# Weight sums of twelve Strassen units made during the attention and kept in DRAM, and five more units by Strassen's scheme

## The chip, the cores and the metric

The kernel runs on one core of a Trainium2 chip. The metric is the device time of one execution in microseconds (us), as the median of several runs. Five engines work beside each other, each through its own instructions in the order of the program: TensorE (PE in the profile; PEld is its weight load), VectorE (DVE), ScalarE (ACT), GpSimd (POOL) and SyncE (SP). An instruction that waits for a semaphore holds up all that stand behind it on its engine. Here SP and POOL do little but issue DMA transfers.

## The reference

One decoder layer on 256 tokens of width 2048, in float32. Two groups of heads attend, their result goes through `w_o`, and a SwiGLU block, a gated embedding and a last norm follow. The change is about the SwiGLU block and borrows time from the attention.

```python
a = rmsnorm(h, attn_norm)
proj = a @ w_in                       # then MLA heads and MoBA heads (causal attention)
h = h + concat(out_mla, out_moba) @ w_o
f = rmsnorm(h, ffn_norm)
h = h + (silu(f @ w_gate) * (f @ w_up)) @ w_down      # D_FF = 5632
g = sigmoid(rmsnorm(h, ple_norm) @ w_ple_gate)
h = h + g * (p @ w_ple_proj)
return rmsnorm(h, final_norm)
```

## The kernel before

**Units.** All large products are cut into units, listed in program order by `group`. A unit is two blocks of 128 rows of a weight (one 1 MB piece of 256 x 1024 in the SwiGLU block) against all 256 tokens. Weights and activations are split into a high and a low part, and `three` (L349) makes each product of three matmuls: high by high, low by high, high by low. An ordinary unit has 2 row blocks x 2 column halves x 2 token halves, each of three matmuls with 512 columns: 24 matmuls. A Strassen unit treats its 256 x 1024 piece of weight and its 256 x 256 piece of activation as two by two quarters and needs seven products instead of eight: 21 matmuls (`seven`, L393). For this it needs four weight sums and four activation sums. The activation sums are made once, in `act_transpose` (L127), for the first `SEVENS` pairs of row blocks. The weight sums are made in place by VectorE for every Strassen unit (`split_lo`, L339, L342 and L343).

**The way of a weight.** SP loads it from DRAM into one of the buffers `raw0` to `raw4` (three of them during the attention, five in the SwiGLU block). ScalarE writes the high part into a ring (`split_hi`, L329; ringh, moreh, most in the profile), VectorE subtracts it from the raw data to get the low part (`split_lo`, L340; ringl, morel, most), TensorE multiplies. A buffer is free again when its last split is done, and a place in the ring when the matmuls that read it are done. So splits stand two units ahead of their matmuls in the attention, and about 11 us ahead in the SwiGLU block.

**Order.** The loop at the end of the kernel writes out the program unit by unit. For each it first calls `step()`, which moves every open task on by one piece (attention heads, norms, transposes), then emits the splits of later units whose ring places are free, then the matmuls. The sequence is: input projections (ga, q0, u0, q1, u1, qk0, qk1, v) with the attention as tasks between them; wo0 and wo1 for `w_o`; then for the five column groups ci = 0 to 4 of the SwiGLU block eight units of gate (g0 to g4) and eight of up (u0 to u4; the label u0 is used by both parts), with the down units of the group before between them; then a narrower group, the last down units, and the gated embedding.

`mixed` (L990) names the pairs of row blocks of a group in their order, with an S ahead of those that go by Strassen's scheme: two in u0, five in g1, six in g2 to g4 and u1 to u4. After the last unit of an up group VectorE adds the Strassen part to each of the four banks and multiplies it with the gate (L381 and L958, "the evacuation" below); the result is then transposed on TensorE (`ff_transpose`, L978). For ci = 1 to 4 these transposes wait in `S["turned"]` until the down units in between are done. For ci = 0 they are a task: half of them stand in the program behind the 24 matmuls of g1's first unit, half one unit later.

Of the kernel before, what the change touches and what calls it, by code (L numbers as in the profile page):

```python
# [8 lines left out]
F32 = mybir.dt.float32  # L9
# [26 lines left out]
def kernel(ctx, tc, x, p, positions, attn_norm, w_in, kv_norm, w_ukv, w_o, ffn_norm,  # L36
# [150 lines left out]
        pass  # L187

    def group(name, srcs, ks, chunks, lhs, evac, pool=None, singles=0, per=2, sums=None, sevens=(), adding=(),
              order=None, swap=False, bank0=0, deep=False, into=None):  # L190

        pairs = [ks[i:i + 1] for i in range(singles)] + [ks[i:i + per] for i in range(singles, len(ks), per)]
        st = {"banks": None, "begun": set()}
        for i, pr in enumerate(pairs):
            u = Unit()
            u.name, u.srcs, u.ks, u.chunks, u.lhs, u.st = name, srcs, pr, chunks, lhs, st
            u.first, u.last, u.evac, u.pool = i == 0, i == len(pairs) - 1, evac, pool
            u.order = order or [(c, t) for c in range(len(chunks)) for t in range(NT)]
            u.idx, u.store, u.again, u.into = i, None, None, into
            u.strassen, u.sevens_first, u.sevens_end = i in sevens, i in sevens[:1], i in sevens[-1:]  # L200
            u.mixed, u.sums, u.swap, u.bank0, u.deep, u.adding = len(sevens) > 0, sums, swap, bank0, deep, i in adding
            units.append(u)

    raw = {}
# [7 lines left out]
    def load(i):  # L212
        if i >= len(units) or units[i].again or i in raw:
            return
        u = units[i]
        u.asked = asking[0]
        n = sum(c1 - c0 for _, c0, c1 in u.srcs)
        nk = len(u.ks)
        if u.raw >= len(raws):
            raws.append(big.tile([128, 2048], F32, name=f"raw{u.raw}", tag=f"f1{'hl'[u.raw - 3]}"))  # L220
# [16 lines left out]
    def plan(wide):  # L237
# [18 lines left out]
            jobs.append(jb)  # L256
            return jb

        order = [0, 1, 2]
        back = next(i for i, u in enumerate(units) if u.name == "dl0")  # L260
        for i, u in enumerate(units):
            u.turns = []
            if u.again:
                continue
            if i == wide:
                at = 12
            if i == wide + 3:
                order = [3, 4] + order
            u.raw = order.pop(0)
            order.append(u.raw)  # L270
            nch, nk = len(u.chunks), len(u.ks)
# [34 lines left out]
        return jb.h, jb.l  # L306

    def raw_of(jb):
        f = raw[jb.unit].rearrange("q k c -> q (k c)")
# [21 lines left out]
    def split_lo(jb, c0=0, c1=None, n=1):  # L331

        if units[jb.unit].adding:
            return
        h, l, r = by_row_tile(n, *parts_of(jb), raw_of(jb))
        tt = nc.vector.tensor_tensor
        f = quarters(jb) if jb.kind == "21" else None
        if f is not None:
            tt(f[:, 0:2], f[:, 1:2].to_broadcast([128, 2, 512]), f[:, 0:4:3], op=ALU.subtract)  # L339
        tt(l[:, :, c0:c1], r[:, :, c0:c1], h[:, :, c0:c1].bitcast(F32), op=ALU.subtract)  # L340
        if f is not None:
            tt(f[:, 3], f[:, 3], f[:, 0], op=ALU.subtract)  # L342
            tt(f[:, 2], f[:, 2], f[:, 3], op=ALU.subtract)  # L343

    def split(jb):
        split_hi(jb)
# [326 lines left out]
    def after_q_mla(half):  # L673
        def g():
# [205 lines left out]
            add(g(), wait)  # L880
        return after

    SEVENS = 6

    def ffn_norm_half(k0):

        def after():
            def g():
                if k0 == 0:
                    S["nrm"] = stage_tile(1024).rearrange("q t (a b) -> q (t a) b", a=2).rearrange(  # L890
                        "q n (u v) -> q n u v", u=2)
                    sums = [big.tile([128, 2, 3, 4, 128], F32R, name=f"sums{x}", tag=x) for x in ("att", "more_sums")]
                    S["sums"] = [[x[:, i, n] for x in sums for n in range(3)] for i in range(2)]
# [59 lines left out]
    def up_evac(ci, n, nb):  # L953
        left = {"n": nb}

        def f(c, t, c0, c1, b, off=0):
# [32 lines left out]

    def mixed(name, order=((0, 0), (1, 0), (0, 1), (1, 1))):  # L990

        pairs = {'g0': '0 1 2 3 4 5 6 7', 'u0': '6 7 S0 S1 2 3 4 5', 'g1': '6 5 S0 S1 S2 S3 S4 7'}.get(name, '6 S0 S1 S2 S3 S4 S5 7').split()
        n = [int(x.strip("S+")) for x in pairs]
        sevens = tuple(i for i, x in enumerate(pairs) if x[0] == "S")
        return dict(ks=[2 * x + i for x in n for i in range(2)], chunks=C2, lhs=a_l, sums=a_sums, sevens=sevens,
                    adding=tuple(i for i, x in enumerate(pairs) if x[-1] == "+"), order=list(order) if sevens else None,
                    swap=not sevens, deep=True)

    def gate(ci):
# [228 lines left out]
        return ahead  # L1228

    nxt, j = 2, 0  # L1230
    for i, u in enumerate(units):
        asking[0] = i
        load(i + 3)
        if i < 5:
            load_x(xt, 768 + 256 * i, 1024 + 256 * i)
        if u.name == "dl0" and u.idx == 1:
# [8 lines left out]
            step()  # L1245
        for n in range(max(1, len(u.turns))):
            todo, late = [], []
            while nxt < len(jobs) and jobs[nxt].wait < j and jobs[nxt].unit <= i + (3 if i > 1 else 1) and \
# [36 lines left out]
            done = jobs[nxt].unit - 1 if nxt < len(jobs) else len(units)  # L1285
            for m in range(i + 4, min(done + 6, len(units)) if i >= wide else min(done + 4, wide + 3)):
                load(m)
            j += not u.again


# [23 lines left out]
```

## Time and profile before

| | us |
|---|---|
| time, median of 3 runs (1191.03 to 1191.93) | 1191.58 |
| the profiled execution, its own time | 1192.75 |
| its span, first to last instruction | 1191.0 |
| TensorE busy in the span | 1179.0 |
| VectorE busy | 916.2 |
| ScalarE busy | 699.7 |
| GpSimd busy | 43.4 |
| data moved by DMA | 250.30 MB |

TensorE counts as busy while a matmul is in its pipeline, so its share says that it hardly ever ran dry, not that it ran at its peak. VectorE is busy for about two thirds of the attention and almost always in the SwiGLU block, as the slices of the page show:

```
PE   9999999999999999999999999999999999999996
DVE  5644635656457678998999899989998999897474
```

In a row of a timeline the columns are the start, the busy time, engine, line, operation, output and inputs with shapes, and in brackets the idle time of the engine before it with what ended it.

### The profile page before, as it was taken

To read this page: it belongs to the slowest core of one execution; us is meant where nothing else is said; L and a number is where in the kernel's file an instruction comes from. 1 tells how busy PE (TensorE), PEld (TensorE's weight loads), DVE (VectorE), ACT (ScalarE), POOL (GpSimd) and SP (SyncE) were. 2 spreads that over 40 slices of the span, in tenths; PEclk is the share of its full clock that TensorE was granted. 3 is DMA by queue.
4 is the path that set the end of the run, shared out by engine and by line. 5 is a ranking of instruction groups with operands and counts; after the bars stand their busy time and mean duration, and the time that the engine had idled before them with its cause. 6 is when DMAs were issued, how large, how long until landed. Compare 5 with 4: busy or idle time off the path is not lost.

```text
span 1191.0 us, 14454 instructions
## 1 busy us (share of the span) xinstructions
PE 1179.0 (99%) x5501; PEld 984.1 (83%) x5501; DVE 916.2 (77%) x1076; ACT 699.7 (59%) x892; POOL 43.4 (4%) x56
## 2 busy tenths in 40 slices
PE   9999999999999999999999999999999999999996
PEld 6888888899888888888888888888888888888886
DVE  5644635656457678998999899989998999897474
ACT  6745645456556755465656565757465656465453
POOL 4300000000000000000000000000000000000000
PEclk9999999999999999999999999999999999999998
DMA  8653654435653877385867777686859586836531
GB/s 295 219 194 110 216 162 166 151 110 199 237 210 119 297 236 269 117 297 167 296 194 243 235 238 238 216 279 201 258 210 281 186 262 213 340 137 220 209 106 71
DMA packets 79734, 250.30 MB, mean 210 GB/s; under 512 B 4844, under 2 KB 9248, under 8 KB 78384
## 3 DMA queue, kind: packets, MB, share of 16 engines
q1 hardware_dynamic: 75744, 229.93, 54.1%
q0 software_dynamic: 3632, 18.93, 8.7%
q8 instruction: 43, 0.70, 0.2%
q10 hardware_dynamic: 288, 0.52, 0.1%
q14 instruction: 27, 0.22, 0.1%
HBM read 228.39 MB, written 12.58 MB: 202 GB/s over the span
## 4 chain that ended last, share of the span: by engine, by line
PE 97%; ACT 1%; DVE 1%; DMA 1%; SPq 0%; issue 0%; DVEq 0%
PE bank L353 31%; PE bank L351 31%; PE bank L352 31%; PE bank L138 1%; PE bank L978 1%; PE bank L542 1%; PE bank L663 1%; DMA x<-in_x 1%; PE bank L571 0%; PE bank L545 0%; PE bank L565 0%; DVE ringl L340 0%; ACT ringh L329 0%; ACT att L555 0%; ACT att L561 0%; PE bank L572 0%
## 5 line engine op out<-in xcount | busy, mean ns | idle before, releaser
L340 DVE TENSOR_TENSOR ringl<-raw,ringh 128x1024 fp32r<-128x1024 f32 (+4 forms) x298 | 436.5, 1483 | 133.9 <-ACT ringh L329 129.4
L329 ACT CAST ringh<-raw 128x1024 fp32r<-128x1024 f32 (+4 forms) x298 | 365.9, 1262 | 282.5 <-PE bank L352 122.9
L351 PE MATMUL bank<-ringh,aT 128*128 128x512 f32 (+3 forms) x744 | 287.4, 386 | 0.0
L353 PE MATMUL bank<-ringl,aT 128*128 128x512 f32 (+3 forms) x744 | 282.9, 380 | 0.1
L352 PE MATMUL bank<-ringh,aT 128*128 128x512 f32 (+3 forms) x744 | 282.1, 379 | 0.0
L353 PEld LDWEIGHTS bank<-ringl,aT 128*128 128x128 f32 x744 | 139.7, 188 | 27.3 <-DVE ringl L340 1.8
L352 PEld LDWEIGHTS bank<-ringh,aT 128*128 128x128 f32 x744 | 140.0, 188 | 24.7
L351 PEld LDWEIGHTS bank<-ringh,aT 128*128 128x128 f32 x744 | 140.0, 188 | 24.6 <-ACT aT L124 0.3
L329 ACT CAST moreh<-raw 128x1024 fp32r<-128x1024 f32 (+2 forms) x68 | 78.9, 1187 | 46.7 <-DVE raw L339 31.9
L340 DVE TENSOR_TENSOR morel<-raw,moreh 128x1024 fp32r<-128x1024 f32 (+2 forms) x64 | 84.1, 1328 | 1.2 <-ACT moreh L329 0.6
L351 PE MATMUL bank<-ringh,ffTh 128*128 128x512 f32 x204 | 79.4, 389 | 0.0
L352 PE MATMUL bank<-ringh,ffTl 128*128 128x512 f32 x204 | 79.4, 389 | 0.0
L353 PE MATMUL bank<-ringl,ffTh 128*128 128x512 f32 x204 | 79.4, 389 | 0.0
L329 ACT CAST most<-raw 128x1024 fp32r<-128x1024 f32 (+2 forms) x55 | 54.3, 1012 | 33.5 <-DVE raw L339 20.6
L339 DVE TENSOR_TENSOR raw<-raw 128x1024 f32<-128x1024 f32 x57 | 69.8, 1225 | 1.9
L340 DVE TENSOR_TENSOR most<-raw,most 128x1024 fp32r<-128x1024 f32 (+2 forms) x55 | 63.9, 1170 | 1.8 <-ACT most L329 1.6
L352 PEld LDWEIGHTS bank<-ringh,ffTl 128*128 128x128 f32 x204 | 38.3, 188 | 8.0
L351 PEld LDWEIGHTS bank<-ringh,ffTh 128*128 128x128 f32 x204 | 38.3, 188 | 7.9
L353 PEld LDWEIGHTS bank<-ringl,ffTh 128*128 128x128 f32 x204 | 38.3, 188 | 7.9
L343 DVE TENSOR_TENSOR raw<-raw 128x512 f32<-128x512 f32 x57 | 39.4, 692 | 2.0
L342 DVE TENSOR_TENSOR raw<-raw 128x512 f32<-128x512 f32 x57 | 39.0, 684 | 0.0
L353 PE MATMUL bank<-most,aT 128*128 128x512 f32 x86 | 33.9, 395 | 0.0
(332 smaller groups left out, 1869.0 us busy)
## 6 DMA issues: line engine op xcount, KB each, us to landing
raw<-in_w_down SPq DMA_DIRECT2D x44, 1024.0 KB, 4.9
raw<-in_w_gate SPq DMA_DIRECT2D x40, 1024.0 KB, 7.0
raw<-in_w_up SPq DMA_DIRECT2D x40, 1024.0 KB, 8.4
raw<-in_w_in SPq DMA_DIRECT2D x40, 512.0 KB, 4.1
raw<-in_w_o SPq DMA_DIRECT2D x16, 1024.0 KB, 5.2
raw<-in_w_ple_gate SPq DMA_DIRECT2D x16, 1024.0 KB, 5.0
raw<-in_w_in SPq DMA_DIRECT2D x8, 1024.0 KB, 4.9
hd<-copied POOLq DMA_DIRECT2D x8, 1024.0 KB, 9.5
```

The lines of the kernel that those rows point to most:

```text
L138: nc.tensor.transpose(b[:, (2 * i + t) * 128:(2 * i + t + 1) * 128], part[:, t, i * 128:(i + 1) * 128], ident)
L329: nc.scalar.copy(h[:, :, c0:c1], r[:, :, c0:c1])
L339: tt(f[:, 0:2], f[:, 1:2].to_broadcast([128, 2, 512]), f[:, 0:4:3], op=ALU.subtract)
L340: tt(l[:, :, c0:c1], r[:, :, c0:c1], h[:, :, c0:c1].bitcast(F32), op=ALU.subtract)
L342: tt(f[:, 3], f[:, 3], f[:, 0], op=ALU.subtract)
L343: tt(f[:, 2], f[:, 2], f[:, 3], op=ALU.subtract)
L351: nc.tensor.matmul(b, xh, h, start=start, stop=False)
L352: nc.tensor.matmul(b, xl, h, start=False, stop=False)
L353: nc.tensor.matmul(b, xh, l, start=False, stop=stop)
L542: nc.tensor.matmul(s[:, c0:c0 + nk], qT[:, q * 128:(q + 1) * 128], kT[:, 0:nk], start=True, stop=qpe is None)
L663: nc.tensor.transpose(b[:, (2 * i + t) * 128:(2 * i + t + 1) * 128], src[:, t, col(i0 + i):col(i0 + i) + 128], ident)
L978: nc.tensor.transpose(b[:, (2 * i + t) * 128:(2 * i + t + 1) * 128], st[:, t, (k + i) * 128:(k + i + 1) * 128], ident)
```

## The change

- **Five more Strassen units.** `SEVENS` is 7, so a seventh pair of row blocks gets activation sums. `mixed` gives g1 six Strassen units and u1 to u4 seven each. The groups u1 to u4 now begin with a Strassen unit.
- **Early sums.** For the last Strassen unit of g1 to g4 and the last two of u1 to u4 (12 units) a new task, `early_sums`, makes the weight sums during the attention. For each unit GpSimd issues a load of the 1 MB piece into one SBUF buffer; three steps later VectorE makes the sums in place with three instructions, and GpSimd issues a store of them to DRAM; one step later the next unit's load follows, which waits for that store. In the SwiGLU block such a unit loads 0.75 MB of the weight and 1 MB of sums into two of the five raw buffers, and its three instructions on VectorE fall away there.
- **Loads.** They are now issued by `loads`, as soon as the splits that used the same buffers before stand in the program.
- **Zeros.** The clearing of `qpT` goes from GpSimd to VectorE.
- **Transposes of ci = 0.** `up_evac` now puts them into `S["mid"]` instead of a task. The loop takes `S["mid"]` up behind the first ordinary unit of a mixed group, and u0's own last unit is one.

```diff
-                if 0 < ci < 5:
-                    S["turned"] = turned
+                if ci < 5:
+                    S["turned" if ci else "mid"] = turned
                 else:
-                    add(turned, 2 if ci else 1)
+                    add(turned, 2)
...
-    SEVENS = 6
+    SEVENS = 7
...
-        pairs = {'g0': '0 1 2 3 4 5 6 7', 'u0': '6 7 S0 S1 2 3 4 5', 'g1': '6 5 S0 S1 S2 S3 S4 7'}.get(name, '6 S0 S1 S2 S3 S4 S5 7').split()
+        pairs = {'g0': '0 1 2 3 4 5 6 7', 'u0': '6 7 S0 S1 2 3 4 5', 'g1': '6 S0 S1 S2 S3 S4 S5 7'}.get(
+            name, '6 S0 S1 S2 S3 S4 S5 7' if name[0] == 'g' else 'S0 S1 S2 S3 S4 S5 S6 7').split()
...
+                    early=sevens[-2 if name[0] == "u" else -1:] if name[-1] in "1234" else (), order=list(order) if sevens else None,
...
+    def early_sums():
+        for u in units:
+            if not u.early:
+                continue
+            f = big.tile([128, 4, 512], F32, name="wsums", tag="more_sums")
+            (w, c0, _), k0 = u.srcs[0], u.ks[0] * 128
+            nc.gpsimd.dma_start(f.rearrange("q (k a) c -> q k (a c)", k=2),
+                                w[k0:k0 + 256, c0:c0 + 1024].rearrange("(k q) c -> q k c", q=128))
+            yield 3
+            tt = nc.vector.tensor_tensor
+            tt(f[:, 0:2], f[:, 1:2].to_broadcast([128, 2, 512]), f[:, 0:4:3], op=ALU.subtract)
+            tt(f[:, 3], f[:, 3], f[:, 0], op=ALU.subtract)
+            tt(f[:, 2], f[:, 2], f[:, 3], op=ALU.subtract)
+            u.early = dram.tile([128, 2048], F32, name=f"wsums{u.name}{u.idx}")
+            nc.gpsimd.dma_start(u.early, f.rearrange("q a c -> q (a c)"))
+            yield 1
...
+        if u.early:
+            r = raws[u.raw][:, 0:1536]
+            (w, c0, _), k0 = u.srcs[0], u.ks[0] * 128
+            nc.sync.dma_start(r[:, 0:512], w[k0:k0 + 128, c0:c0 + 512])
+            nc.sync.dma_start(r[:, 512:1536], w[k0 + 128:k0 + 256, c0:c0 + 1024])
+            nc.sync.dma_start(raws[u.raw2], u.early)
...
-                nc.gpsimd.memset(qpT[64 - 64 * i:128 - 64 * i, i::2], 0.0)
+                nc.vector.memset(qpT[64 - 64 * i:128 - 64 * i, i::2], 0.0)
```

**TensorE behind u0 of the SwiGLU block.** Before, these rows stand behind the 24 matmuls of g1's first unit: L978 is the transpose of ci = 0, bank the PSUM bank that is written.

```order
L351 MATMUL bank_82<-ringh,aT_85 128x512
L352 MATMUL bank_82<-ringh,aT_86 128x512
L353 MATMUL bank_82<-ringl,aT_85 128x512
L978 MATMUL bank_77<-ident,stage 128x128 x4
L978 MATMUL bank_78<-ident,stage 128x128 x4
L351 MATMUL bank_83<-ringh,aT_85 128x512
L352 MATMUL bank_83<-ringh,aT_86 128x512
```

Now, in the changed program, the last matmuls of u0 (from the buffer most) and the first of g1 (bank_83) look so; the transposes have line L1019.

```order
L390 MATMUL bank_80<-most,aT_85 128x512
L391 MATMUL bank_80<-most,aT_86 128x512
L392 MATMUL bank_80<-most,aT_85 128x512
L1019 MATMUL bank_77<-ident,stage 128x128 x4
L1019 MATMUL bank_78<-ident,stage 128x128 x4
L1019 MATMUL bank_79<-ident,stage 128x128 x4
L1019 MATMUL bank_80<-ident,stage 128x128 x4
L390 MATMUL bank_83<-ringh,aT_85 128x512
```

All sixteen transposes moved from behind g1's first unit (and the next) to directly behind u0's last matmul.

**VectorE ahead of u0's evacuation.** Before: raw_113 and raw_114 hold g1's first two units, raw_2794 its third, which is its first Strassen unit; L381 begins the evacuation.

```order
L340 TENSOR_TENSOR ringl<-raw_113,ringh 128x1024 x2
L340 TENSOR_TENSOR ringl<-raw_114,ringh 128x1024 x2
L340 TENSOR_TENSOR ringl<-raw_2794,ringh 128x1024
L339 TENSOR_TENSOR raw_2794<-raw_2794 128x1024
L340 TENSOR_TENSOR ringl<-raw_2794,ringh 128x512
L342 TENSOR_TENSOR raw_2794<-raw_2794 128x512
L343 TENSOR_TENSOR raw_2794<-raw_2794 128x512
L340 TENSOR_TENSOR morel<-raw_2794,moreh 128x1024 x2
L381 TENSOR_TENSOR U<-U,bank_77 128x512
```

Now, with L361 for the split, L360, L363 and L364 for the sums and L420 for the evacuation, behind the first unit's pair of splits:

```order
L361 TENSOR_TENSOR ringl<-raw_114,ringh 128x1024
L360 TENSOR_TENSOR raw_114<-raw_114 128x1024
L361 TENSOR_TENSOR ringl<-raw_114,ringh 128x512
L363 TENSOR_TENSOR raw_114<-raw_114 128x512
L364 TENSOR_TENSOR raw_114<-raw_114 128x512
L361 TENSOR_TENSOR ringl<-raw_114,ringh 128x1024 x2
L361 TENSOR_TENSOR morel<-raw_2910,moreh 128x1024
L360 TENSOR_TENSOR raw_2910<-raw_2910 128x1024
L361 TENSOR_TENSOR morel<-raw_2910,moreh 128x512
L363 TENSOR_TENSOR raw_2910<-raw_2910 128x512
L364 TENSOR_TENSOR raw_2910<-raw_2910 128x512
L420 TENSOR_TENSOR U<-U,bank_77 128x512
```

The second unit of g1 has become a Strassen unit, so a whole Strassen unit and most of the next stand ahead of the evacuation, instead of an ordinary unit and one Strassen unit.

**VectorE at the change from v to wo0.** In the changed program the sums of the eleventh early unit (L377 to L379) stand between the splits of wo0's first unit (raw_114) and its second (raw_112); L587 is the first step of an attention head.

```order
L361 TENSOR_TENSOR ringl<-raw_114,ringh 128x2048
L377 TENSOR_TENSOR wsums<-wsums 128x1024
L378 TENSOR_TENSOR wsums<-wsums 128x512
L379 TENSOR_TENSOR wsums<-wsums 128x512
L361 TENSOR_TENSOR ringl<-raw_112,ringh 128x2048
L587 SCALAR_TENSOR_TENSOR att<-bank_83,mask 128x384
L592 TENSOR_REDUCE nm<-att 128x1 x2
```

Nothing else moved there; the three rows are new.

More of the change, by code (lines that the diff above doesn't have):

```diff
@@ L189, in group @@
     def group(name, srcs, ks, chunks, lhs, evac, pool=None, singles=0, per=2, sums=None, sevens=(), adding=(),
-              order=None, swap=False, bank0=0, deep=False, into=None):
+              order=None, swap=False, bank0=0, deep=False, into=None, early=()):
         pairs = [ks[i:i + 1] for i in range(singles)] + [ks[i:i + per] for i in range(singles, len(ks), per)]
@@ L201, in group @@
             u.mixed, u.sums, u.swap, u.bank0, u.deep, u.adding = len(sevens) > 0, sums, swap, bank0, deep, i in adding
+            u.early = i in early
             units.append(u)
@@ L216, in load @@
         u.asked = asking[0]
+        while max(u.raw, u.raw2) >= len(raws):
+            n = len(raws)
+            raws.append(big.tile([128, 2048], F32, name=f"raw{n}", tag=f"f1{'hl'[n - 3]}"))
+        if u.early:
[4 more added lines that the diff above has]
+            nc.sync.dma_start(raws[u.raw2], u.early)
+            raw[i] = r.rearrange("q (a c) -> q a c", a=3)
+            return
         n = sum(c1 - c0 for _, c0, c1 in u.srcs)
         nk = len(u.ks)
-        if u.raw >= len(raws):
-            raws.append(big.tile([128, 2048], F32, name=f"raw{u.raw}", tag=f"f1{'hl'[u.raw - 3]}"))
         r = raws[u.raw][:, 0:nk * n].rearrange("q (k c) -> q k c", k=nk)
@@ L257, in job @@
             return jb
-        order = [0, 1, 2]
+        order, user = [0, 1, 2], {}
         back = next(i for i, u in enumerate(units) if u.name == "dl0")
@@ L270, in plan @@
             order.append(u.raw)
+            u.raw2 = -1
+            if u.early:
+                u.raw2 = order.pop(0)
+                order.append(u.raw2)
+            u.behind = max(user.get(x, -1) for x in (u.raw, u.raw2))
+            for x in (u.raw, u.raw2):
+                if x >= 0:
+                    user[x] = i
             nch, nk = len(u.chunks), len(u.ks)
@@ L308, in raw_of @@
     def raw_of(jb):
+        if units[jb.unit].early:
+            r, s = raw[jb.unit], raws[units[jb.unit].raw2]
+            return {"11 22": r[:, 0:3:2], "21": r[:, 1], "t1 t3": s[:, 0:1024], "t4 t2": s[:, 1024:2048]}[jb.kind]
         f = raw[jb.unit].rearrange("q k c -> q (k c)")
@@ L336, in split_lo @@
         tt = nc.vector.tensor_tensor
-        f = quarters(jb) if jb.kind == "21" else None
+        f = quarters(jb) if jb.kind == "21" and not units[jb.unit].early else None
         if f is not None:
@@ L892, in g @@
                     sums = [big.tile([128, 2, 3, 4, 128], F32R, name=f"sums{x}", tag=x) for x in ("att", "more_sums")]
-                    S["sums"] = [[x[:, i, n] for x in sums for n in range(3)] for i in range(2)]
+                    last = [big.tile([128, 4, 128], F32R, name="sums6h", tag="tabs"),
+                            work.tile([128, 4, 128], F32R, name="sums6l", tag="ra", bufs=1)]
+                    S["sums"] = [[x[:, i, n] for x in sums for n in range(3)] + [last[i]] for i in range(2)]
                     S["rs"] = make_rstd(ssh[:, :, 0:2], D // 2, "rs")
@@ L995, in mixed @@
         return dict(ks=[2 * x + i for x in n for i in range(2)], chunks=C2, lhs=a_l, sums=a_sums, sevens=sevens,
-                    adding=tuple(i for i, x in enumerate(pairs) if x[-1] == "+"), order=list(order) if sevens else None,
+                    adding=tuple(i for i, x in enumerate(pairs) if x[-1] == "+"),
+                    early=sevens[-2 if name[0] == "u" else -1:] if name[-1] in "1234" else (), order=list(order) if sevens else None,
                     swap=not sevens, deep=True)
@@ L1230, with loads @@
     nxt, j = 2, 0
+    coming = 3
+    def loads(end):
+        nonlocal coming
+        while coming < end and (units[coming].again or units[coming].behind < (
+                jobs[nxt].unit if nxt < len(jobs) else len(units))):
+            load(coming)
+            coming += 1
     for i, u in enumerate(units):
         asking[0] = i
-        load(i + 3)
+        if i < wide:
+            load(i + 3)
+        if u.name == "q0" and u.idx == 0:
+            add(early_sums())
         if i < 5:
@@ L1247 @@
             todo, late = [], []
-            while nxt < len(jobs) and jobs[nxt].wait < j and jobs[nxt].unit <= i + (3 if i > 1 else 1) and \
+            while i not in raw and u.turns:
+                loads(i + 1)
+            while nxt < len(jobs) and jobs[nxt].unit in raw and jobs[nxt].wait < j and jobs[nxt].unit <= i + (3 if i > 1 else 1) and \
                     (jobs[nxt].unit <= i + 2 or i >= wide and units[jobs[nxt].unit].asked < i) and \
@@ L1284 @@
                 split_lo(jb)
-            done = jobs[nxt].unit - 1 if nxt < len(jobs) else len(units)
-            for m in range(i + 4, min(done + 6, len(units)) if i >= wide else min(done + 4, wide + 3)):
-                load(m)
+            loads(len(units) if i >= wide else wide + 3)
             j += not u.again
```

## The prediction

> **What bounds the kernel now.** I read the busy shares first, then the waits of TensorE, then the spacing of its matmuls.
>
> ```profile
> span 1191.0 us, 14454 instructions
> PE 1179.0 (99%) x5501; PEld 984.1 (83%) x5501; DVE 916.2 (77%) x1076; ACT 699.7 (59%) x892; POOL 43.4 (4%) x56
> PE bank L113 <- DVE junk L108: 2.0, 1, 2.0
> PE bank L138 <- DMA x<-in_x: 0.9, 1, 0.9
> PEld bank L353 <- DVE ringl L340: 2.5, 8, 0.5
> PEld bank L353 <- DVE most L340: 1.0, 4, 0.3
> ```
>
> A row of the waits gives engine, line and releaser, then microseconds in total, times, and the longest. TensorE itself waits only in the first microseconds, and its weight loads wait 3.5 us in twelve places. So TensorE bounds the kernel, and an instruction taken from it is a gain only as long as nothing makes it wait. The matmul's price is the pitch, not its listed duration, since matmuls overlap:
>
> ```profile
> 473.88 0.39 PE L353 MATMUL bank<-most,aT 128*128 128x512 f32 x1
> 474.11 0.39 PE L351 MATMUL bank<-ringh,aT 128*128 128x512 f32 x1
> 479.55 1.03 PE L978 MATMUL bank<-ident,stage 128*128 128x128 f32 x8
> 480.34 0.48 PE L351 MATMUL bank<-ringh,aT 128*128 128x512 f32 x1
> ```
>
> Between 474.11 and 479.55 stand the 24 matmuls of g1's first unit: 5.44 / 24 = 0.227 us each. Eight transposes take 480.34 - 479.55 = 0.79 us.
>
> The sum is made against the profiled execution, 1192.75 us, which is 1.75 over its span and 1.17 over the median of 1191.58; I add the same difference to the median.
>
> **Five units by Strassen's scheme.** Each saves 24 - 21 = 3 matmuls: 5 x 3 x 0.227 = **-3.4 us** on TensorE. That is all that the change takes from the bounding engine.
>
> **Sums out of the SwiGLU block.**
>
> ```profile
> L339 DVE TENSOR_TENSOR raw<-raw 128x1024 f32<-128x1024 f32 x57 | 69.8, 1225 | 1.9
> L343 DVE TENSOR_TENSOR raw<-raw 128x512 f32<-128x512 f32 x57 | 39.4, 692 | 2.0
> L342 DVE TENSOR_TENSOR raw<-raw 128x512 f32<-128x512 f32 x57 | 39.0, 684 | 0.0
> ```
>
> The sums of one unit cost VectorE 1.225 + 0.684 + 0.692 = 2.6 us. Twelve leave the block where VectorE is nearly full, five come in with the new units; seven net are 18 us of VectorE, off TensorE's path. They pay only through waits that go, and those are small:
>
> ```profile
> 632.39 0.39 PE L352 MATMUL bank<-ringh,sumsmore_sums 128*128 128x512 f32 x1
> 632.77 0.50 PE L353 MATMUL bank<-ringl,sumsmore_sums 128*128 128x512 f32 x1
> ```
>
> Here the next matmul starts 0.38 us after the last one, 0.15 over the pitch. Twelve such are 1.8 at most, and several of them lie outside g1 to u4 or beside ordinary units; I take **-0.5** (0 to -1.3).
>
> **Transposes behind u0.** They now stand straight behind u0's last matmul, so TensorE reaches them at 474.11, and each needs the evacuation of its bank by VectorE. Before, g1's first unit covered that. When does VectorE come to it?
>
> ```profile
> 461.40 5.76 DVE L340 TENSOR_TENSOR ringl<-raw,ringh 128x1024 fp32r<-128x1024 f32 x5
> 467.19 1.23 DVE L339 TENSOR_TENSOR raw<-raw 128x1024 f32<-128x1024 f32 x1
> ...
> 470.26 2.51 DVE L340 TENSOR_TENSOR morel<-raw,moreh 128x1024 fp32r<-128x1024 f32 x2
> 472.68 0.68 DVE L381 TENSOR_TENSOR U<-U,bank 128x512 f32<-128x512 f32 x1
> ...
> 476.17 0.75 DVE L958 SCALAR_TENSOR_TENSOR stage<-U,rf,stage 128x512 f32<-128x512 f32 x1
> 477.55 0.75 DVE L958 SCALAR_TENSOR_TENSOR stage<-U,rf,stage 128x512 f32<-128x512 f32 x1
> ...
> 488.98 1.21 DVE L339 TENSOR_TENSOR raw<-raw 128x1024 f32<-128x1024 f32 x1
> 495.71 1.22 DVE L339 TENSOR_TENSOR raw<-raw 128x1024 f32<-128x1024 f32 x1
> ```
>
> VectorE has no idle time there. The five splits take 1.15 each, so the two of g1's first unit end at 463.7. By the order, a whole Strassen unit follows: consecutive ones stand 495.71 - 488.98 = 6.73 apart, which gives 470.4. Then come the next unit's first split (1.15) and its middle (467.19 to 470.26, 3.07): the evacuation starts at about 474.65 instead of 472.68. It ran in the order of the banks; the third was done 476.17 + 0.75 - 472.68 = 4.24 after its start, the fourth 5.62 after. That gives 478.9 and 480.3. The first eight transposes read the first and the third bank, the others the second and the fourth: eight start at 478.9 and end at 479.7, eight start at 480.3 and end at 481.1. Unhindered, sixteen would end at 474.11 + 1.58 = 475.7. So TensorE loses **+5.4**. The lower end is **0.85**: even if VectorE came early, the fourth bank's add and product, 477.55 - 476.17 = 1.38 by the spacing of the rows, can't begin before u0's last matmul has ended at 474.3, so the last eight transposes end at 474.3 + 1.38 + 0.79 = 476.5 instead of 475.7. Behind the waiting transposes on TensorE stands all of g1; VectorE and ScalarE then meet matmuls that are 5 us late, and nothing of that is owed again.
>
> **The clock after this gap.** TensorE would be idle from 474.3 to 478.9, 4.6 us, which before has nowhere but at its ends.
>
> ```profile
> 2.01 1.89 PE L113 MATMUL bank<-junk 128*128 128x512 bf16 x4 [2.01 <-DVE junk L108]
> 7.10 0.40 PE L352 MATMUL bank<-ringh,aT 128*128 128x512 f32 x1
> 7.33 0.40 PE L353 MATMUL bank<-ringl,aT 128*128 128x512 f32 x1
> ...
> 1182.00:1184.00 2.00, 0.01 (x1) 0.00 (x0) 1.35 (x5) 1.93 (x3) 0.00 (x0) 1.00 0.00 0
> 1184.00:1186.00 2.00, 0.00 (x0) 0.00 (x0) 1.90 (x9) 0.58 (x3) 0.00 (x0) 0.65 0.00 0
> ```
>
> In the windows the columns are the stretch, its length, the busy time of PE, PEld, DVE, ACT and POOL, the granted clock, the share of DMA and GB/s. TensorE ended at 1182.0; the mean clock of 1184 to 1186 is 0.65, so at half speed it fell at 1184.6, 2.6 us after. At the start four matmuls took 1.89 us, 0.47 each, twice the pitch, and by 7.10 to 7.33 the pitch is 0.23: full speed came some 5 us after the first work at 2.01. By these rows a gap of 4.6 us lowers the clock, and then 5 us run at half speed and lose 2.5. Part of these 5 us is the waiting between the two halves of the transposes, so I take **+2.0** (0 to 2.5, since one fall at the program's end is thin evidence).
>
> [...]
>
> **Early sums in the attention.** For each of twelve units GpSimd loads 1 MB, VectorE works 2.6 us, GpSimd stores 1 MB, and the next load waits for that store in GpSimd's queue. The three instructions on VectorE wait for the load, and the splits behind them wait as well. How long does the load take beside the others?
>
> ```profile
> raw<-in_w_o SPq DMA_DIRECT2D x16, 1024.0 KB, 5.2
> hd<-copied POOLq DMA_DIRECT2D x8, 1024.0 KB, 9.5
> ...
> 280.00:282.00 2.00, 2.00 (x18) 2.00 (x17) 0.54 (x1) 2.00 (x3) 0.00 (x0) 1.00 1.04 401
> 282.00:284.00 2.00, 2.00 (x16) 2.00 (x15) 1.75 (x1) 0.78 (x2) 0.00 (x0) 1.00 0.97 393
> ```
>
> SP's 1 MB takes 5.2 us; GpSimd's, which adds while it writes, 9.5. Plain transfers from GpSimd aren't in the trace; I take 6.5, nearer to the plain row, since the engines are full there (share 0.97 to 1.04). So two sums should stand at least 13 + 2.6 us apart. Two places are closer.
>
> *v to wo0.* The order puts the eleventh sums between two splits of w_o, the tenth behind the RECIPROCAL here:
>
> ```profile
> 270.31 0.15 DVE L559 RECIPROCAL ri<-sm 128x2 f32<-128x2 f32 x1
> ...
> 281.46 2.29 DVE L340 TENSOR_TENSOR ringl<-raw,ringh 128x2048 fp32r<-128x2048 f32 x1 [3.39 <-ACT ringh L329]
> 286.18 2.29 DVE L340 TENSOR_TENSOR ringl<-raw,ringh 128x2048 fp32r<-128x2048 f32 x1 [2.42 <-ACT ringh L329]
> ...
> 288.56 0.57 DVE att L548
> ...
> 304.72 0.37 ACT pTb L566
> ...
> 305.14 0.70 PE bank L571 x2
> ```
>
> The tenth end at 270.4 + 2.6 = 273.0; store and load bring the eleventh's piece at 286.0; its sums end at 288.6, and the split planned for 286.18 is 2.4 late. Behind it stand the attention steps from 288.56 on. The last two rows are from the chain that ended last: from 288.56 to 305.14 it runs through VectorE and ScalarE to TensorE's next matmul, so the delay reaches TensorE: **+2.4**. With 5.2 us a transfer the piece lands at 283.4, in VectorE's idle time, and the price is 0.1; with 9.5 it lands at 292 and costs 8.
>
> *q1.* The sums ahead of the two splits below stand only 15 us apart.
>
> ```profile
> 111.24 1.22 DVE L340 TENSOR_TENSOR ringl<-raw,ringh 128x1024 fp32r<-128x1024 f32 x1 [8.41 <-ACT ringh L329]
> 127.49 1.22 DVE L340 TENSOR_TENSOR ringl<-raw,ringh 128x1024 fp32r<-128x1024 f32 x1
> ```
>
> They need 15.6 and 2.6 for themselves; by the timelines of both engines the second split ends 2.8 us ahead of its matmul. That leaves about **+0.4** (0 to 2).
>
> **Costed at nothing.** The seventh pair's activation sums (VectorE has over 7 us in hand there), the zeros on VectorE (about 1 us, 6 in hand), the last sums at 304 (6 in hand), 12 x 0.75 MB more of loads in the SwiGLU block and fewer free raw buffers: a 1 MB load takes 5 to 8 us and splits are 11 ahead. If that cover goes, each of twelve units could cost a microsecond.
>
> **The sum:** -3.4 - 0.5 + 5.4 + 2.0 + 2.4 + 0.4 = **+6.3**: 1199.0 for the profiled execution, **1197.9** for the median.
>
> **The rivals.**
>
> *The clock stays up.* All else as above, without 2.0: **1195.9**. For it speaks that the one fall in the trace is at the end of the program, where work may count otherwise: if the fall needs a stretch of idle time that a gap in the middle doesn't fill, nothing is slowed. [...] 20 in 100.
>
> *The sums in the attention hide.* Transfers of 5.2 us and VectorE's idle 3.39 and 2.42 us take them in: without 2.4 and 0.4, **1195.1**. Against it stand the full DMA engines. 15 in 100; with the clock up as well, **1193.1**, 4 in 100.
>
> *Slow transfers.* At 9.5 us each v to wo0 costs 8 instead of 2.4: **1203.5**; twelve late raw pieces would give about as much. 13 in 100.
>
> *VectorE comes in time (the other side).* The transposes wait only for the last bank, 0.85, and no clock falls. This decides if the evacuation starts by about 472.5, two microseconds ahead of my count, as it would if VectorE did one Strassen unit's splits less than the order puts ahead of it or were ahead by as much. With the attention hidden too: -3.4 - 0.5 + 0.85 + 0.1 = -3.0, **1188.6**. Against it stands that VectorE is full from 454 to 478. 9 in 100. The -3.4 itself I hardly doubt, since the rows that TensorE loses are in the order.
>
> **How the numbers follow.** The forecast has 39 in 100, with its own range of 1196 to 1200.5 (TensorE's small waits, 2.0 and 0.4 at their ends). Faster or slower by 0.2%, 2.4 us, is about what a measurement of this kernel can tell from no change: below 1189.2 or above 1194.0. Faster is the last rival, 9; within are the double case and the low edges of its neighbours, 15; slower 76. The range of 1193.5 to 1203.0 leaves out the last rival and most of the slow transfers.
>
> **What would show it.** TensorE's waits for VectorE on the lines of the transposes, 4 to 5 us plus 0.6, at about 474 plus the shift till there; a granted clock of about one half in a few microseconds from there; the eleventh sums ending at 288 or later, and the matmul of L571's kind 2 us late against the matmuls ahead of it; 5183 order rows on TensorE and no new waits from u1 to u4. Wrong it would be if the evacuation starts ahead of u0's last matmul, or if late pieces make TensorE wait in many units.

## The result, and the profile after

| | before | changed |
|---|---|---|
| time, median of 4 runs each, us | 1191.76 | 1200.36 (1199.77 to 1202.29) |
| ratio, with its 95% interval | | 1.0075 (1.0057 to 1.0092) |
| profiled execution / its span | 1192.75 / 1191.0 | 1199.77 / 1198.0 |

The change made the kernel 8.6 us slower; 6.3 had been forecast. The pages of the profiled executions, 7.0 us apart, hold the reason; the one of the changed kernel is the shortest of its four. First the busy times of the changed kernel, and TensorE's waits (engine, line, releaser; total us, times, longest):

```profile
PE 1176.4 (98%) x5486; PEld 984.2 (82%) x5486; DVE 939.6 (78%) x1109; ACT 709.6 (59%) x904; POOL 55.0 (5%) x76
PE bank L1019 <- DVE stage L999: 4.4, 2, 2.4
PE bank L610 <- DVE att L587: 2.8, 1, 2.8
PE bank L390 <- ACT stage L850: 1.6, 1, 1.6
PE bank L610 <- ACT pTb L605: 1.0, 1, 1.0
PE bank L392 <- DVE ringl L361: 0.4, 1, 0.4
```

TensorE has 15 matmuls fewer (5486 against 5501), as the change says. But where before it waited for nobody after the first microseconds, there are now six waits of 10.2 us together. Next the places, from the timelines of TensorE and VectorE:

```profile
139.81 0.50 PE L390 MATMUL bank<-ringh,ckvT 128*128 128x512 f32 x1 [1.63 <-ACT stage L850]
...
295.06 0.48 PE L610 MATMUL bank<-pTb,vb 128*128 128x256 f32 x1 [2.76 <-DVE att L587]
...
310.94 0.48 PE L610 MATMUL bank<-pTb,vb 128*128 128x256 f32 x1 [1.05 <-ACT pTb L605]
...
479.64 0.39 PE L392 MATMUL bank<-most,aT 128*128 128x512 f32 x1
482.02 0.33 PE L1019 MATMUL bank<-ident,stage 128*128 128x128 f32 x1 [1.99 <-DVE stage L999]
484.79 3.35 PE L1019 MATMUL bank<-ident,stage 128*128 128x128 f32 x15 [2.44 <-DVE stage L999]
487.90 0.48 PE L390 MATMUL bank<-ringh,aT 128*128 128x512 f32 x1
```

```profile
128.97 1.23 DVE L377 TENSOR_TENSOR wsums<-wsums 128x1024 f32<-128x1024 f32 x1 [2.12 <-DMA wsums<-in_w_gate]
...
289.66 1.23 DVE L377 TENSOR_TENSOR wsums<-wsums 128x1024 f32<-128x1024 f32 x1 [1.73 <-DMA wsums<-in_w_up]
...
480.50 0.68 DVE L420 TENSOR_TENSOR U<-U,bank 128x512 f32<-128x512 f32 x1
```

At 128.97 and 289.66 VectorE stands still for a load of GpSimd's, with splits and attention steps behind it in its queue. At 480.50 the evacuation begins 0.6 us after u0's last matmul has ended; the first transpose waits for the first bank, the others for the third. The 15 transposes behind the second wait take 3.1 us to g1's first matmul, 0.21 each instead of the 0.10 of before. The windows show the clock (columns as in the prediction; it is the last but two):

```profile
482.00:484.00 2.00, 0.33 (x1) 0.14 (x1) 1.93 (x4) 0.00 (x0) 0.00 (x0) 1.00 0.00 0
484.00:486.00 2.00, 1.21 (x6) 1.21 (x7) 1.97 (x3) 0.27 (x1) 0.00 (x0) 0.62 0.00 0
486.00:488.00 2.00, 2.00 (x12) 2.00 (x11) 1.50 (x3) 1.47 (x3) 0.00 (x0) 0.53 0.00 0
488.00:490.00 2.00, 2.00 (x11) 1.68 (x10) 1.64 (x3) 1.84 (x4) 0.00 (x0) 1.00 0.00 0
```

Up to u0's end both programs have the same matmuls in the same order, so the start of one in both traces gives the delay so far. The steps in it, in us:

| place in the changed trace | term forecast | step measured |
|---|---|---|
| first 10 us, the load of x | none | -0.7 (the wait for x: 0.9 before, 0.3 now) |
| 139.8, end of q1 | +0.4 | +1.9 |
| 278, v | none | +0.6 |
| 295.1, v to wo0 | +2.4 | +3.0 |
| 310.9, the end of the same chain | part of the +2.4 | +1.0 |
| 479.6 to 487.9, transposes: waits | +5.4 | +4.8 |
| the same, half clock | +2.0 | +1.6 |
| 15 matmuls, counted, at 0.227 each | -3.4 | -3.4 |
| small waits of the SwiGLU block | -0.5 | -1.7 |
| sum | +6.3 | +7.1 |

The stretch at the transposes is 487.90 - 479.64 = 8.26 us, where sixteen transposes and a matmul take 1.58 + 0.23 = 1.81 without a wait. The row of the small waits is what remains to the last matmul, which starts 7.1 us later than before; TensorE's weight loads wait for VectorE's splits less than before, three times for 1.4 us instead of twelve times for 3.5:

```profile
PEld bank L392 <- DVE ringl L361: 1.4, 3, 0.6
```

The chain that ended last in the changed trace ties the two rows of v to wo0 together:

```profile
292.25 2.29 DVE ringl L361
294.54 0.48 DVE att L587
...
310.94 0.70 PE bank L610 x2
```

It is the chain that the prediction names, from VectorE's step at 288.56 to TensorE's matmul at 305.14. VectorE begins it 4.2 us later than before (294.54 - 288.56, less the 1.8 of the rows above), and TensorE meets the delay in two waits: 3.0 at the matmul of 290.33 before, which needs the bank that the first attention step reads, and 1.0 at its end.

### The profile page after: what moved, and what is told of

Same layout as the page of the kernel before. It is cut to its first block, busy times and chain, and to the rows that moved or that the text cites. A ratio compares the mean times of both kernels' runs of the same rounds, so it can differ in the third digit from the quotient of the medians.

```text
span 1198.0 us, 14599 instructions
## 1 busy us (share of the span) xinstructions
PE 1176.4 (98%) x5486; PEld 984.2 (82%) x5486; DVE 939.6 (78%) x1109; ACT 709.6 (59%) x904; POOL 55.0 (5%) x76
## 4 chain that ended last, share of the span: by engine, by line
PE 82%; DVE 4%; DMA 2%; ACT 2%; issue 1%; DVEq 0%; ACTq 0%
PE bank L390 26%; PE bank L392 26%; PE bank L391 26%; DVE ringl L361 1%; PE bank L1019 1%; DMA raw<-in_w_o 1%; DMA wsums<-in_w_gate 1%; PE bank L138 1%; ACT ringh L350 1%; PE bank L610 0%; ACT att L594 0%; ACT att L600 0%; DVE wsums L377 0%; PE bank L702 0%; DVE nm L592 0%
## 5 line engine op out<-in xcount | busy, mean ns | idle before, releaser
L350 ACT CAST ringh<-raw 128x1024 fp32r<-128x1024 f32 (+4 forms) x303 | 370.7, 1259 | 269.9 <-PE bank L391 122.3
L361 DVE TENSOR_TENSOR ringl<-raw,ringh 128x1024 fp32r<-128x1024 f32 (+4 forms) x301 | 437.0, 1475 | 113.8 <-ACT ringh L350 109.2
L390 PE MATMUL bank<-ringh,aT 128*128 128x512 f32 (+3 forms) x721 | 278.5, 386 | 0.0
L392 PE MATMUL bank<-ringl,aT 128*128 128x512 f32 (+3 forms) x721 | 274.0, 380 | 0.5 <-DVE ringl L361 0.4
L391 PE MATMUL bank<-ringh,aT 128*128 128x512 f32 (+3 forms) x721 | 273.5, 379 | 0.0
L392 PEld LDWEIGHTS bank<-ringl,aT 128*128 128x128 f32 x721 | 135.5, 188 | 26.0 <-DVE ringl L361 1.4
L390 PEld LDWEIGHTS bank<-ringh,aT 128*128 128x128 f32 x721 | 135.8, 188 | 23.7 <-ACT aT L124 0.3
L391 PEld LDWEIGHTS bank<-ringh,aT 128*128 128x128 f32 x721 | 135.7, 188 | 23.6
L361 DVE TENSOR_TENSOR morel<-raw,moreh 128x1024 fp32r<-128x1024 f32 (+2 forms) x68 | 87.5, 1306 | 5.1 <-ACT moreh L350 4.6
L350 ACT CAST most<-raw 128x1024 fp32r<-128x1024 f32 (+2 forms) x58 | 57.7, 1021 | 37.1 <-DVE raw L360 15.1
L361 DVE TENSOR_TENSOR most<-raw,most 128x1024 fp32r<-128x1024 f32 (+2 forms) x58 | 67.6, 1183 | 2.6 <-ACT most L350 2.4
L360 DVE TENSOR_TENSOR raw<-raw 128x1024 f32<-128x1024 f32 x50 | 61.3, 1225 | 1.7
L390 PE MATMUL bank<-moreh,aT 128*128 128x512 f32 x92 | 36.0, 392 | 0.0
L364 DVE TENSOR_TENSOR raw<-raw 128x512 f32<-128x512 f32 x50 | 34.6, 692 | 1.7
L392 PE MATMUL bank<-morel,aT 128*128 128x512 f32 x92 | 35.9, 390 | 0.0
```

The costliest lines, as they stand in the source:

```text
L350: nc.scalar.copy(h[:, :, c0:c1], r[:, :, c0:c1])
L390: nc.tensor.matmul(b, xh, h, start=start, stop=False)
L391: nc.tensor.matmul(b, xl, h, start=False, stop=False)
L392: nc.tensor.matmul(b, xh, l, start=False, stop=stop)
```

## The experiments

Each was compared with the kernel before on the same chip, in its own runs. First one part of the change at a time.

**Transposes behind g1's first unit again.** Two rows move the moment; all else is as in the change.

```diff
-                    S["turned" if ci else "mid"] = turned
+                    S["turned" if ci else "later"] = turned
...
+            if u.name == "g1" and u.idx == 0 and n == len(u.turns) - 1:
+                list(S.pop("later"))
```

> The changed kernel with one thing undone: the sixteen transposes of ci = 0 stand behind the 24 matmuls of g1's first unit again. Theory (the stall behind u0 is VectorE's evacuation being late, and the half clock that follows): in the changed kernel TensorE lost 2.15 + 2.66 us of waiting and 1.6 us of slow transposes there. All of it goes, since the third bank is done 4.8 us and the fourth 6.2 us after u0's last matmul and 5.4 us of work stand in between: 1200.4 - 6.4 = 1194.0 us, and no window near 480 shows a clock under 1.00. Rival (VectorE is behind in any case, and the wait only moves to g1's first Strassen unit or to the transposes): at most half of it goes, 1197 or more.

Measured: 1196.18 us, ratio 1.0041 (1.0028 to 1.0053). Of the 6.4 us forecast 4.2 came, so both theories hold a part. The timeline of TensorE, with the 24 matmuls ahead of the transposes:

```profile
484.34 1.91 PE L1019 MATMUL bank<-ident,stage 128*128 128x128 f32 x16
489.20 0.50 PE L390 MATMUL bank<-ringh,aT 128*128 128x512 f32 x1 [2.95 <-DVE ffTl L122]
```

The transposes themselves no longer wait. But the next unit is now a Strassen unit, which needs the PSUM banks that the transposes wrote, and VectorE takes those up at 488.46, behind the rest of the evacuation and three splits. The stall moved one step on and became shorter. The order of g1 itself, not the place of the transposes alone, has to go back.

**Transposes early in the kernel before.** The kernel before, with only the edit of `up_evac`:

```diff
-                if 0 < ci < 5:
-                    S["turned"] = turned
+                if ci < 5:
+                    S["turned" if ci else "mid"] = turned
```

> The kernel before with one part of the change alone: the transposes of ci = 0 directly behind u0's last matmul; VectorE's order ahead of the evacuation stays as before. Theory (each bank's transposes wait for its evacuation): the evacuation starts at 472.7, the third bank is done at 476.9, the fourth at 478.3; the transposes end at about 479.2 instead of 475.7, +3.4 us: 1195.2; TensorE idles for about 2.6 us. If a gap of that length also lowers the clock, as at the end of the trace of before, up to 1.6 more: 1196.8. Rival (only the order of VectorE, a Strassen unit more ahead of the evacuation, makes the stall): nearly nothing but the last bank, +0.9, 1192.7.

Measured: 1194.57 us, ratio 1.0026 (1.0015 to 1.0036), +2.9 for the +3.4 of the theory without the clock. TensorE waits 2.7 us on the transposes, and the clock stays up:

```profile
474.00:476.00 2.00, 0.00 (x0) 0.00 (x0) 1.93 (x3) 0.00 (x0) 0.00 (x0) 1.00 0.97 393
476.00:478.00 2.00, 1.49 (x12) 1.25 (x13) 1.96 (x4) 1.07 (x2) 0.00 (x0) 1.00 0.19 76
```

So a little under half of the price at this place comes from the transposes' new place, and the rest from VectorE's later evacuation: with it the waits are 4.4 us instead of 2.7, and the clock fell as well. (Behind the wait of 2.44 us here it stayed at 1.00; in the changed kernel it fell to 0.50 during the second of two waits, 1.99 and 2.44 us, with one transpose between them. The last section has both.)

**The five units without early sums**, transposes behind g1's first unit:

```diff
-                    early=sevens[-2 if name[0] == "u" else -1:] if name[-1] in "1234" else (), order=list(order) if sevens else None,
+                    order=list(order) if sevens else None,
```

> The changed kernel without the early sums (their load, sums and store in the attention, and the loads of sums in the SwiGLU block, are gone; the five new units make their sums on VectorE as all others do) and with the transposes behind g1's first unit. Theory (the early sums aren't needed to make the five units pay): TensorE is shorter by 15 x 0.227 = 3.4 us, the attention is as before, and VectorE, busy for 508 of 540 us in the SwiGLU block before, takes 13 us more with some small waits: 1188.4 to 1190.5. Rival (VectorE is full and each new unit's 2.6 us of sums end up as waits of TensorE): 13 us less 3.4, or most of it, 1195 to 1201.

Measured: 1208.4 us, ratio 1.0141 (1.0127 to 1.0155): the theory fell, and the rival was too low. Against the first experiment, which differs in the early sums alone, it is 12.2 us slower, though the attention runs as before. Its waits:

```profile
PE bank L392 <- DVE ringl L361: 5.5, 5, 1.2
PE bank L392 <- DVE morel L361: 3.5, 3, 1.2
PE bank L390 <- DVE ffTl L122: 3.0, 1, 3.0
PE bank L392 <- DVE most L361: 2.0, 2, 1.1
```

TensorE waits for low parts, 11.0 us in ten places, in most groups from u1 on. Before, VectorE had next to nothing free there, as this window of the kernel before shows (DVE is the third busy time):

```profile
550.00:600.00 50.00, 50.00 (x221) 41.20 (x220) 49.03 (x52) 28.75 (x29) 0.88 (x1) 1.00 0.72 242
```

Here a Strassen unit more needs 2.6 us more of it in 3 matmuls' less time, and that time becomes TensorE's. The early sums are thus what the five units need: against the first experiment this trace is 5.5 us ahead at the end of the attention and 10.9 behind at the last matmul, so in the SwiGLU block they are worth 16.4 us. The zeros on VectorE and the new order of the loads, which this run keeps, cost the attention nothing.

**The early sums alone**, on the pairs and the transposes of before:

```diff
-    SEVENS = 7
+    SEVENS = 6
...
-        pairs = {'g0': '0 1 2 3 4 5 6 7', 'u0': '6 7 S0 S1 2 3 4 5', 'g1': '6 S0 S1 S2 S3 S4 S5 7'}.get(
-            name, '6 S0 S1 S2 S3 S4 S5 7' if name[0] == 'g' else 'S0 S1 S2 S3 S4 S5 S6 7').split()
+        pairs = {'g0': '0 1 2 3 4 5 6 7', 'u0': '6 7 S0 S1 2 3 4 5', 'g1': '6 5 S0 S1 S2 S3 S4 7'}.get(name, '6 S0 S1 S2 S3 S4 S5 7').split()
```

> The changed kernel without the five new units and with the transposes as before: what is left of the change is the early sums of twelve units, the loads of them and the zeros on VectorE. Theory (the waits in the attention come from the early sums): between 110 and 310 us TensorE starts 1.9 us later at 139, 0.6 at 276, 3.0 at 290 and 1.0 at 305, together 6.5, and the SwiGLU block gains at most 1.5 of its small waits: 1196.5 to 1198.5. Rival (it is another part, such as the zeros or the seventh pair, that delays the attention): no more than 2 us, 1190 to 1193.8.

Measured: 1196.69 us, ratio 1.0045 (1.0031 to 1.0058), as the theory has it. The steps stand at the same matmuls: 3.0 us at 139, 0.6 at 276 and 2.9 at 290, and from 305 to the end 1.6 us come back. (The profiled execution, 1199.89 us, is the longest of its runs; its granted clock fell behind each of the two large waits, to 0.50 in the window of 142 to 144 us and 0.52 in that of 298 to 300. The fall behind 290 cost next to nothing: at the end of the chain the delay is 4.2 us, against 4.0 in the changed kernel, where the clock is 1.00 from 294 to 300.)

**Two sums left out on VectorE**, the fourth and the eleventh unit's:

```diff
+            if len(at) not in (4, 11):
                 tt(f[:, 0:2], f[:, 1:2].to_broadcast([128, 2, 512]), f[:, 0:4:3], op=ALU.subtract)
                 tt(f[:, 3], f[:, 3], f[:, 0], op=ALU.subtract)
                 tt(f[:, 2], f[:, 2], f[:, 3], op=ALU.subtract)
```

> The changed kernel with VectorE's three instructions left out for the fourth and the eleventh early unit (their loads and stores stay, so the sums of two units are missing from the result). It asks whether VectorE's order or the extra transfers delay the attention. Theory (VectorE's order): both waits go, 1.9 us at 139 and 3.0 at 290, with what hangs on them 1195 to 1196. Rival (the transfers): the second piece of w_o landed at 289.8 in the changed kernel, after 10.4 us beside GpSimd's load instead of 5.2, and ScalarE's split of it ended at 291.8, only 0.5 us before VectorE was free; then the wait at 139 goes but at least 2 us of that at 290 stay, 1198 to 1199.

Measured: 1197.08 us, ratio 1.0041 (1.0026 to 1.0057). The wait at 139 is gone, all 1.9 us of it: there VectorE's order was the cause. At 290 the step is 2.5 of the former 3.0, so there the rival holds; at the end of the chain it is 3.5 of 4.0. The chain that ended last (start, us, what), first of the changed kernel, then of this run:

```profile
279.39 10.38 DMA raw<-in_w_o
...
289.87 1.90 ACT ringh L350
...
292.25 2.29 DVE ringl L361
```

```profile
277.08 10.30 DMA raw<-in_w_o
...
287.48 1.91 ACT ringh L350
...
289.41 2.29 DVE ringl L361
```

In both the second piece of `w_o` decides, 10.3 us on its way. In the trace of before the same piece took 8.3, from 275.6.

**The last two units left out** divides this further:

```diff
+            if len(done) == 10:
+                u.early = done[-1].early
+                continue
+            done.append(u)
```

> The changed kernel with the eleventh and the twelfth early unit left out altogether (no load, no sums, no store; their places in the SwiGLU block read the sums of the tenth, so the result lacks theirs). It divides the wait of 2.9 us at 290 into its shares. In the run without the eleventh's instructions on VectorE 2.4 us of it stayed: the w_o piece was issued some 2 us late, since the tenth's sums stand ahead of the splits that free its buffer, and landed 9.9 us after its issue instead of 8.0. Theory (the transfer beside it is the larger part, the issue the smaller): the piece lands within 8.5 us, and the wait falls to 0.5 to 1.2 us; 1197 to 1198.5. Rival (the late issue alone makes the wait): it stays at 2 us or more, 1199 or more.

Measured: 1197.12 us, ratio 1.0045 (1.0028 to 1.0061), in the theory's range. But the four executions lie between 1196.06 and 1200.82, and the profiled one is the longest, with a granted clock of 0.60 and 0.55 in the windows of 140 to 142 and 142 to 144 us and a wait of 1.1 us for a load at 727, so the steps of its trace say more than the time. The transfers of that one issue, as the tile's own view gives them for the changed kernel and for this run:

```profile
L235 SPq DMA_DIRECT2D raw<-in_w_o x1: 368/368/368, 279.4 to 279.4; - x1
...
DMA to landing us min/median/max: 10.4/10.4/10.4
```

```profile
L235 SPq DMA_DIRECT2D raw<-in_w_o x1: 368/368/368, 281.1 to 281.1; - x1
...
DMA to landing us min/median/max: 7.6/7.6/7.6
```

Without GpSimd's load beside it the piece takes 7.6 us, and the wait at 290 is gone altogether. The late issue stays: 281.1 less TensorE's delay of 3.5 is 2.0 us behind the 275.6 of before. It costs 0.8 us at the end of the chain, within what the theory said. So of the 4.0 us of the chain, 0.8 go with the late issue, 2.7 with the transfers of the last two units and 0.5 with the eleventh sums on VectorE.

**The first group as before**, `'g1': '6 5 S0 S1 S2 S3 S4 7'` and the transposes as a task, everything else as in the change, so four new units:

> The changed kernel with the order of g1 and the place of the transposes as before: four new units (u1 to u4) instead of five, early sums kept. Theory (the stall near 480 in the changed kernel, and its shifted form when only the transposes are moved back, come from g1's second unit being a Strassen unit, which needs VectorE for 6.7 us ahead of the evacuation and all banks behind it): no wait of TensorE between 470 and 500, 1200.4 - 6.4 + 0.7 for three matmuls = 1194.7. Rival (late VectorE shows up elsewhere in g1): 1196.5 or more.

Measured: 1194.74 us, ratio 1.0024 (1.0015 to 1.0033), where the theory had 1194.7; that they agree so closely is luck, since the eleven executions lie between 1192.85 and 1197.63. In the profiled one no wait is left between 470 and 500, and the clock there is 1.00. What is left of the loss is the attention.

**The sums placed otherwise**, on top of that: the distances of each load and its sums, in steps, become a list.

```diff
+        waits = [2, 2, 2, 2, 5, 2, 2, 2, 2, 2, 2, 2]
...
-            yield 3
+            yield waits.pop(0)
```

> As the kernel with four new units, with the early sums placed otherwise in VectorE's order: two steps behind each load instead of three, five for the fifth unit; by the order they then stand where the changed kernel's trace had 66, 83, 97, 115, 137, 156, 175, 193, 215, 235, 250 and 267 us, none between v and w_o and none while a load is under way. Theory (the waits of the attention hang on two places only): they go, 1191.7 - 2.7 for twelve matmuls - 1.5 for the small waits of the SwiGLU block, 1187.5 to 1189.5. Rival (any 2.6 us of VectorE and any 2 MB of transfers in the attention cost TensorE about half a microsecond): 1192 or more.

> As the run with the sums earlier, but six steps for the fifth unit: sums at 66, 83, 97, 115, 141, 162, 181, 203, 221, 239, 257 and 274 us by the order; nothing is left of them between 115 and 139 us, and the last store stands beside the first loads of w_o. Theory (q1 is the place that has no room): up to 1 us faster than with five steps, 1187 to 1189. Rival (the last store beside the loads of w_o delays them): 1 to 2 us slower than with five steps.

Measured with five: **1188.86 us, ratio 0.9974 (0.9963 to 0.9984)**, faster than both kernels. With six: 1191.89, ratio 0.9996 (0.9987 to 1.0005). TensorE's waits with five, then with six:

```profile
PE bank L611 <- ACT pTb L606: 1.1, 1, 1.1
PE bank L393 <- DVE ringl L361: 0.3, 1, 0.3
```

```profile
PE bank L703 <- DVE stage L565: 1.7, 1, 1.7
PE bank L611 <- ACT pTb L606: 0.9, 1, 0.9
PE bank L393 <- DVE ringl L361: 0.9, 2, 0.6
```

The waits at 139 and 290 are gone in both, so most of the loss in the attention hung on places, not on VectorE's work or the transfers as such: with five 1.7 us are left of the 6.5 of the changed kernel, 0.7 near 275 and 1.0 at the end of the chain. The time with five lies in the theory's range. That six are slower is what the rival had, but by 3.0 us and for another reason: the twelfth sums stand at 272.7 ahead of the steps on `stage` that the transposes of L703 need at 276, and TensorE waits for VectorE, not for `w_o`.

## Why the prediction was right, and where not

- **What bounds the kernel** held: only 15 matmuls could be gained, and everything else depended on whether they brought waits. VectorE had even more room in the attention than the text ahead of the change says: by the windows of before it was busy for 173.9 of the first 310 us, 56%, not two thirds. The loss came from where the sums stood, not from a lack of room.
- **The transposes** held in mechanism and size. VectorE began 0.1 us later than worked out, relative to u0's last matmul. The waits came to 4.8 us for 5.4, because the second half no longer had to wait: at half clock the first half ended after the fourth bank was ready.
- **The clock** fell as forecast and cost 1.6 us for 2.0. The sum had up to 5 us at half speed, as at the start of the kernel; it was 3.41, from 484.48 to 487.89, with 15 transposes in it. The rival of a clock that stays up fell.
- **q1** was under-sized, 1.9 for 0.4. The place and the mechanism were right. The store ahead of GpSimd's load took less than the 6.5 us of the sum (the load was issued 4.8 after it), but the load took 9.4, as the chain of the changed kernel shows, so VectorE stood still until 128.97 where I had the sums just fit:

```profile
119.43 9.44 DMA wsums<-in_w_gate
```

- **v to wo0** is the step that failed, in its cause and its size: 4.0 us for 2.4. The path from VectorE to TensorE was right. But I had let VectorE's sums push a split that was otherwise due at 286.18, as if its raw piece were there. The runs showed that the piece itself came late, issued 2.0 us later and slowed beside GpSimd's load, and that the sums add only 0.5. The sum took GpSimd's load as slowed by SP's and left SP's at its old time, and it left out that the tenth sums hold up the splits that free SP's buffer.
- **278, v**, was not in the sum, and it has the same root: the tenth sums were placed behind the RECIPROCAL, but the split behind them was not priced. It came at 276.42, and TensorE waited for it:

```profile
271.58 1.21 DVE L377 TENSOR_TENSOR wsums<-wsums 128x1024 f32<-128x1024 f32 x1
...
276.42 1.48 DVE L361 TENSOR_TENSOR ringl<-raw,ringh 128x1280 fp32r<-128x1280 f32 x1
...
277.96 0.41 PE L392 MATMUL bank<-ringl,aT 128*128 128x320 f32 x1 [0.35 <-DVE ringl L361]
```

- **Small waits** were under-sized, -1.7 for -0.5. Without the early sums the same units made 11.0 us of waits for low parts, so VectorE was nearer to being the bound than twelve short waits of the weight loads showed.
- **The other rivals.** Sums that hide in the attention fell, and so did VectorE in time: its evacuation began 0.6 us after u0's last matmul. Slow transfers held by half: GpSimd's eleventh load took 10.7 us, but the store ahead of it 4.4, 15.1 together between the 13 of the sum and the 19 of the rival. (One plain transfer of GpSimd's was in the trace of before, 2 MB in 9.9 us.)
- **The total** is nearer than its parts, and that is luck: the attention was too small by 1.5 + 1.6 + 0.6 = 3.7 us, and the transposes, the clock, the small waits and the start too large by 0.6 + 0.4 + 1.2 + 0.7 = 2.9.
- Of the 8.6 us between the medians the pair of traces explains 7.1. Of the rest, 1.0 is that the profiled execution of before was slower than its median, and 0.6 that the changed one was faster than its own. The changed kernel's other three executions had a mean granted clock of 0.992 to 0.993 against the 0.996 of the profiled one. A stretch of 3.41 us at 0.50, as at 484.48, takes 0.0014 off the mean of 1198 us, so this would be two or three more such stretches: an estimate, since these executions have no trace.

## What to carry to other kernels

Work moved out of a full stretch into an idle one costs nothing only where it fits between the waits of the idle stretch: place it by the chain that ends last there, not by the engine's mean share. Both transfers are priced when one is added beside an urgent one: here the second piece of `w_o` took 10.4 us beside GpSimd's load and 7.6 without it. An instruction whose cover is the unit behind it can't be moved ahead of that unit, and when that unit changes its kind, its needs for buffers and banks come with it.

## What the runs showed of the hardware

**Where the granted clock fell, and for how long.** In the changed trace full speed begins at 6.61 us and falls at 484.48, 477.87 later; the clock is 0.50 for 3.41 us, and 1.00 again for 703.15, until it falls at 1191.04, behind the last matmul. In the trace of before there is one stretch at full speed, 1177.60 us from 7.01 to 1184.61. These four lengths are 140, 1, 206 and 345 times 3.413 us. So windows of 3.41 us are shown here, first two pairs in which the first window ends at a fall: the changed kernel at the transposes, then the run without the last two units at 140 us:

```profile
481.07:484.48 3.41, 0.33 (x1) 0.14 (x1) 3.30 (x6) 0.00 (x0) 0.00 (x0) 1.00 0.00 0
484.48:487.89 3.41, 3.10 (x15) 3.10 (x16) 2.98 (x5) 1.63 (x3) 0.00 (x0) 0.50 0.00 0
```

```profile
136.98:140.39 3.41, 1.43 (x8) 1.04 (x7) 3.38 (x7) 3.41 (x10) 0.71 (x1) 1.00 1.05 401
140.39:143.80 3.41, 3.41 (x9) 2.65 (x9) 3.17 (x15) 3.23 (x8) 0.00 (x0) 0.50 1.05 405
```

And two pairs without a fall: the second experiment at its wait of 2.44 us, and the changed kernel at the 2.76 us of 295.

```profile
471.70:475.12 3.42, 2.08 (x9) 1.29 (x8) 3.35 (x6) 0.00 (x0) 0.00 (x0) 1.00 0.66 189
475.12:478.53 3.41, 2.02 (x16) 1.78 (x17) 3.34 (x6) 1.42 (x3) 0.00 (x0) 1.00 0.37 151
```

```profile
289.92:293.33 3.41, 2.38 (x14) 1.99 (x13) 3.34 (x4) 3.41 (x5) 0.55 (x1) 1.00 0.96 364
293.33:296.75 3.42, 1.69 (x8) 1.47 (x9) 3.35 (x8) 1.50 (x6) 0.00 (x0) 1.00 0.94 337
```

In the first pairs TensorE was idle for 3.08 and 1.98 us of the window that ends at the fall. In the others it was idle for 1.34 and 1.39, and for 1.03 and 1.73 us, and the clock stayed at 1.00. Behind the last matmuls the clock fell as well, at 1184.61 in the trace of before, where TensorE was idle for 2.60 us of the window of 1181.19 to 1184.60, and at 1191.04 in the changed one, where it was idle for 1.92 us of that of 1187.62 to 1191.03.

So the length of a wait alone did not decide in these traces: the clock fell behind the 2.0 us of the run without the last two units, which lie within one of the windows shown, and not behind 2.44 and 2.76, which lie across two. Eight windows set no limit, and what other waits would do is not shown.

The spread of the times goes with the mean granted clock. The kernel with the first group as before, with waits of 0.8 and 2.9 us left, took 1192.85 to 1197.63: 1192.85 at 0.997 and 0.998, 1194.11 to 1195.15 at 0.996, 1196.53 to 1197.63 at 0.995. With the sums earlier, where the longest wait is 1.1, the times lie within 1.4 us, at 0.997 and 0.998.

The fall in the changed kernel cost 1.6 us (15 transposes took 3.1 us instead of 1.5), and so did that in the first experiment, where nine steps from matmul to matmul took 3.65 us instead of 2.04. In the run without the last two units the windows of 140 to 142 and 142 to 144 us, at 0.60 and 0.55, hold 6 matmuls each; in the changed kernel, at 1.00, they hold 10 each.
